# Loading and splitting the first quarter of the weights in two chunks of 128 rows

## The chip, the cores and the metric

The kernel runs on one core of one Trainium2 chip, as one launch. The metric is the device time of a run in microseconds. The median of three runs of the kernel before is 843.33 us (843.28 to 843.36). A profiled execution of the same program, taken on the same kind of chip, is what the trace shows.

## The reference, cut to what matters

Two transformer blocks are computed one after the other on 256 tokens of width 1024, all in float32. The part that the change touches is the very start: an RMS norm of the input, and the first of the products with `w_in`, a 1024 x 6144 matrix.

```python
h = concat([meta_tokens, x])                # 16 + 256 rows of 1024
a = rms_norm(h, norm_mix)
(q_na, k_na, v_na, q_hg, z_f, z_b, i_hg, g_hg, gate_na, gate_hg) = split_cols(a @ w_in)
...                                         # attention, HGRN2, gates, MLP, then two more layers
```

The first product that the kernel makes is `g_hg`, 512 columns of `w_in` that begin at column 3584.

## The kernel before, in words

Every product of the kernel is made in three matmuls on operands cut into a high and a low part: a float32 array is copied to the type float32r (the high part, a Copy on ScalarE) and the rest is the difference (the low part, a subtraction on VectorE). Weights come in units of 512 rows x 512 columns, 1 MB each, in a tile `raw` of 128 partitions x 2048 (four chunks of 128 rows side by side). `emit_raw` loads units in order on SyncE's queue (three `raw` tiles). `emit_hl` splits half a unit at a time, that is two chunks, 128 x 1024: L256 writes `whi`, L257 writes `wlo`. So a quarter of the product `g_hg`, which takes two units, is one such half. `use` hands the chunks to the matmuls.

`xstat` makes, for chunk k of the weights, the matmuls of L351 (high part of the activations, `xh`, with `whi`), L352 (`xh` with `wlo`) and L353 (low part, `xl`, with `whi`), 512 columns each. In the first unit `gh` this is done for the tokens 0 to 127 over chunks 0 to 3, then for the tokens 128 to 255 over the same chunks, then so for chunks 4 to 7.

Ahead of it stands the norm. `norm_in` squares the rows on ScalarE (L443), forms the root on GpSimd (L435) and scales on VectorE (L546). `split_in(t, g)` transposes 4 blocks of 128 x 128 of token tile t and column half g on TensorE (L411) and splits the result into `xh` (ScalarE, L418) and `xl` (VectorE, L419). The code calls these in this order:

```python
norm_in(0, h[0], 2)
first_split(1)            # half unit 0 (the first quarter): L256, L257
x00 = split_in(0, 0)
first_split(2)            # half unit 1
norm_in(1, h[1], 1, x00[:1])
split_in(1, 0)
first_split(3)
x01 = split_in(0, 1)
first_split(4)
split_in(1, 1)
```

The instructions of the whole program are then put in order by a planner, engine by engine, from priorities (the order of the code, with offsets) and a model of their durations. What it makes of a program can be seen only in a trace. The loads at the start are issued on SyncE's queue in the order of the code: the first half of `h[0]` (rows 0 to 127 of x), `grow`, its second half, `ident`, then half unit 0 (L518), `h[1]` (L519, rows 128 to 255 of x), half unit 1 (L520), half units 2 and 3 (L226), and small tables (L525 to L527), before the third unit (L226 again).

Of the kernel before, what the change touches and what calls it, by code (L numbers as in the profile page):

```python
# [11 lines left out]
AF = mybir.ActivationFunctionType  # L12
ALU = mybir.AluOpType
# [57 lines left out]
def kernel(  # L71
# [5 lines left out]
    vecs, cst, out, dbg=None,  # L77
):
    nc = tc.nc
    V, S, T, G = nc.vector, nc.scalar, nc.tensor, nc.gpsimd  # L80
# [12 lines left out]
    def nm(s):  # L93
        uid[0] += 1
        return f"{s}_{uid[0]}"
# [28 lines left out]
    def f(ap):  # L124
        return ap.bitcast(F32)
# [28 lines left out]
    units = []  # L154
# [63 lines left out]
    def emit_raw(n):  # L218
        while st["raw"] < min(n, len(units)):
            i = st["raw"]  # L220
            t = rawp.tile([128, 2048], F32, name=nm("raw"), tag="raw")
            src = units[i][1]
            d = t.rearrange("p (k n) -> p k n", n=src.shape[2])

            for k in (slice(0, 2), slice(2, 4)) if i < QD else (slice(None),):
                raw_ins[:] = [nc.sync.dma_start(out=d[:, k], in_=src[:, k])]  # L226
            raw_t[i] = t
            st["raw"] += 1


    for key, tags in BORROW.items():
        i = [u[0] for u in units].index(key)
# [10 lines left out]
    def emit_hl(i0):  # L243

        while st["hl"] < min(2 * len(units), cap[0]):
            i = st["hl"]
            if i not in borrowed and sum(k not in borrowed for k in range(i0, i)) >= NHL:
                break
            emit_raw(i // 2 + 1)
            r = raw_t[i // 2][:, 1024 * (i % 2):1024 * (i % 2) + 1024]  # L250
            if i in borrowed:
                hi, lo = (slot.tile([128, 2, 512], F32R, name=nm("wb"), tag=g) for g in borrowed[i])
            else:
                hi = hlp.tile([128, 2, 512], F32R, name=nm("whi"), tag="whi")
                lo = hlp.tile([128, 2, 512], F32R, name=nm("wlo"), tag="wlo")
            S.activation(out=hi.rearrange("p k n -> p (k n)"), in_=r, func=AF.Copy)  # L256
            V.tensor_tensor(out=lo.rearrange("p k n -> p (k n)"), in0=r,  # L257
                            in1=f(hi.rearrange("p k n -> p (k n)")), op=ALU.subtract)
            hl_t[i] = (hi, lo)
            st["hl"] += 1  # L260

# [70 lines left out]
    def use(key, budget=None):  # L332

        i = st["use"]
        assert units[i][0] == key, (units[i][0], key)
        with after(behind):
            emit_hl(2 * i)
        behind.clear()
        emit_raw(max(i, st["hl"] // 2 - NHL // 2) + NRAW)
        st["use"] += 1  # L340
        bg_step(budget or base[0], base[1])
        q = [hl_t.pop(2 * i), hl_t.pop(2 * i + 1)]
        return [(q[k // 2][0][:, k % 2], q[k // 2][1][:, k % 2]) for k in range(4)]
# [171 lines left out]
        T.matmul(g_ps[k], lhsT=one_row, rhs=grow[:, 512 * k:512 * k + 512], start=True, stop=True)  # L515
    w0 = rawp.tile([128, 2048], F32, name="raw0", tag="raw")
    w0v = w0.rearrange("p (k n) -> p k n", n=512)
    nc.sync.dma_start(out=w0v[:, 0:2], in_=units[0][1][:, 0:2])  # L518
    nc.sync.dma_start(out=h[1], in_=x[128:256])  # L519
    nc.sync.dma_start(out=w0v[:, 2:4], in_=units[0][1][:, 2:4])  # L520
    raw_t[0] = w0
# [32 lines left out]
    def first_split(n):  # L554
        cap[0] = n
        emit_hl(0)
        cap[0] = 1 << 30
# [36 lines left out]
    with after(raw_ins):  # L594
# [8 lines left out]
                    in0=vc[:, R_LB:R_LB + 16].rearrange("p (d l h) -> p d l h", d=2, l=2)[:, :, 0],  # L603
                    in1=vc[:, R_LB:R_LB + 16].rearrange("p (d l h) -> p d l h", d=2, l=2)[:, :, 1], op=ALU.subtract)
# [411 lines left out]
    for n in range(2):  # L1016
        ws = use(("yn", n))
        for t in range(2):
# [3 lines left out]
            c = slice(512 * n, 512 * n + 512)  # L1022
# [3 lines left out]
    for n in range(2):  # L1026
        ws = use(("yh", n))
        nl = len(later)
        for t in range(2):
# [3 lines left out]
            c = slice(512 * n, 512 * n + 512)  # L1033
# [331 lines left out]
    for g in range(4):  # L1365
        ps = mps()
        for b in range(2):
            for c in range(2):
                i = 2 * g + c
# [7 lines left out]
        for b in range(2):  # L1377
            k = 2 * g + b
# [353 lines left out]
```

## Time and profile before

| what | value |
|---|---|
| median of three runs | 843.33 us |
| the profiled execution, its own time | 843.46 us |
| its span, from the first to the last instruction | 841.6 us |
| TensorE (PE) busy | 827.7 us, 98% of the span |
| VectorE (DVE) busy | 577.8 us, 69% |
| ScalarE (ACT) busy | 466.6 us, 55% |
| mean rate of the DMA engines | 199 GB/s |

The profiled execution takes 1.86 us more than its span, which lies before the first and behind the last instruction. Times inside a trace count from the start of the span. A busy TensorE is not a TensorE at its peak: its matmuls overlap, so the distance from one start to the next tells more than the duration of one.

### The profile page before, as it was taken

What the parts mean: (1) busy time and instruction counts of PE and PEld (TensorE: products, weight loads), DVE (VectorE), ACT (ScalarE), POOL (GpSimd) and SP (SyncE); (2) the same over time, 40 slices, a digit from 0 to 9 for tenths busy, and PEclk for the clock granted to TensorE, in tenths of its full rate; (3) what the DMA queues carried; (4) which work ended last, traced back from release to release, by engine and by line L of the source; (5) the groups of instructions that cost most, each with busy time, mean ns of one, the idle gap of its engine ahead of it and who ended that gap; (6) DMA issues with size and microseconds to landing.
All of it is one profiled execution on the core that took longest, in us unless ns stands there. A gap on an engine that the chain in (4) does not pass through costs nothing.

```text
span 841.6 us, 13162 instructions
## 1 busy us (share of the span) xinstructions
PE 827.7 (98%) x5181; PEld 741.5 (88%) x5181; DVE 577.8 (69%) x832; ACT 466.6 (55%) x769; POOL 58.9 (7%) x139
## 2 busy tenths in 40 slices
PE   7999999999999999999999999999999999999996
PEld 5999998888889999999879989888799999898885
DVE  5746667775849976657976777876655557559753
ACT  6456755574556655544775546545566455555442
POOL 2420020001000000000021000000000000020001
PEclk9999999999999999999999999999999999999999
DMA  8863443442549997868737656757155444468521
GB/s 306 258 200 101 151 151 101 162 154 85 200 129 367 370 335 274 300 210 286 256 98 250 201 179 223 248 201 246 62 209 172 150 154 170 172 220 301 176 78 50
DMA packets 88104, 167.51 MB, mean 199 GB/s; under 512 B 4793, under 2 KB 8889, under 8 KB 88043
## 3 DMA queue, kind: packets, MB, share of 16 engines
q1 hardware_dynamic: 87371, 166.13, 57.6%
q8 instruction: 40, 0.66, 0.3%
q10 hardware_dynamic: 288, 0.52, 0.2%
q14 instruction: 21, 0.17, 0.1%
q0 software_dynamic: 384, 0.03, 0.0%
HBM read 165.62 MB, written 1.05 MB: 198 GB/s over the span
## 4 chain that ended last, share of the span: by engine, by line
PE 93%; DVE 2%; DMA 1%; ACT 1%; issue 1%; POOL 0%; SPq 0%; POOLq 0%; DVEq 0%; ACTq 0%
PE acc L353 15%; PE acc L351 15%; PE acc L352 15%; PE acc L363 9%; PE acc L362 9%; PE acc L361 9%; PE mp L363 3%; PE mp L361 3%; PE mp L362 3%; PE mp L411 2%; PE mp L881 1%; DMA raw<-in_w_in_dram 1%; PE mp L353 1%; PE mp L351 1%; DMA raw<-in_even_in_w_dram 1%
## 5 line engine op out<-in xcount | busy, mean ns | idle before, releaser
L257 DVE TENSOR_TENSOR wlo<-raw,whi 128x1024 fp32r<-128x1024 f32 x244 | 293.9, 1224 | 139.8 <-ACT whi L256 137.6
L256 ACT ACTIVATE whi<-raw 128x1024 fp32r<-128x1024 f32 x244 | 251.0, 1055 | 148.3 <-PE acc L353 90.0
L478 DVE SCALAR_TENSOR_TENSOR tb<-adw,csil,tb 128x512 f32<-128x512 f32 x96 | 71.1, 748 | 11.1 <-issue 5.8
L363 PE MATMUL acc<-oh,wlo 128*128 128x256 f32 x256 | 73.3, 287 | 0.0
L362 PE MATMUL acc<-ol,whi 128*128 128x256 f32 x256 | 73.0, 285 | 0.0
L361 PE MATMUL acc<-oh,whi 128*128 128x256 f32 x256 | 72.7, 284 | 0.0
L362 PE MATMUL acc<-xl,whi 128*128 128x272 f32 (+1 forms) x224 | 64.6, 288 | 0.0
L363 PE MATMUL acc<-xh,wlo 128*128 128x272 f32 (+1 forms) x224 | 64.5, 289 | 0.0
L361 PE MATMUL acc<-xh,whi 128*128 128x272 f32 (+1 forms) x224 | 64.3, 289 | 0.0
L361 PE MATMUL mp<-uh,whi 128*128 128x256 f32 x224 | 63.1, 285 | 0.0
L362 PE MATMUL mp<-ul,whi 128*128 128x256 f32 x224 | 63.0, 283 | 0.0
L363 PE MATMUL mp<-uh,wlo 128*128 128x256 f32 x224 | 62.1, 283 | 0.0
L351 PE MATMUL acc<-whi,hh 128*128 128x512 f32 x128 | 50.0, 392 | 0.0
L352 PE MATMUL acc<-wlo,hh 128*128 128x512 f32 x128 | 49.9, 390 | 0.0
L362 PEld LDWEIGHTS acc<-ol,whi 128*128 128x128 f32 x256 | 49.0, 191 | 0.9 <-issue 0.8
L353 PE MATMUL acc<-whi,hl 128*128 128x512 f32 x128 | 49.7, 390 | 0.0
L363 PEld LDWEIGHTS acc<-oh,wlo 128*128 128x128 f32 x256 | 49.0, 192 | 0.2
L361 PEld LDWEIGHTS acc<-oh,whi 128*128 128x128 f32 x256 | 49.0, 191 | 0.2
L351 PE MATMUL acc<-whi,yT 128*128 128x512 f32 (+1 forms) x128 | 48.5, 379 | 0.0
L352 PE MATMUL acc<-wlo,yT 128*128 128x512 f32 (+1 forms) x128 | 48.3, 377 | 0.0
L353 PE MATMUL acc<-whi,yT 128*128 128x512 f32 (+1 forms) x128 | 48.2, 377 | 0.0
L362 PEld LDWEIGHTS mp<-ul,whi 128*128 128x128 f32 x224 | 42.9, 192 | 0.1
(414 smaller groups left out, 2002.7 us busy)
## 6 DMA issues: line engine op xcount, KB each, us to landing
raw<-in_odd_in_w_dram SPq DMA_DIRECT2D x28, 1024.0 KB, 5.0
adw<-in_ada_w_dram SPq DMA_DIRECT2D x48, 512.0 KB, 6.1
raw<-in_w_in_dram SPq DMA_DIRECT2D x21, 1024.0 KB, 5.2
raw<-in_even_in_w_dram SPq DMA_DIRECT2D x20, 1024.0 KB, 5.1
raw<-in_w_up_dram SPq DMA_DIRECT2D x16, 1024.0 KB, 6.5
raw<-in_w_down_dram SPq DMA_DIRECT2D x16, 1024.0 KB, 7.3
raw<-in_even_out_w_dram SPq DMA_DIRECT2D x8, 1024.0 KB, 5.1
raw<-in_odd_out_w_dram SPq DMA_DIRECT2D x8, 1024.0 KB, 4.9
```

What stands on the lines that cost most here:

```text
L256: S.activation(out=hi.rearrange("p k n -> p (k n)"), in_=r, func=AF.Copy)
L257: V.tensor_tensor(out=lo.rearrange("p k n -> p (k n)"), in0=r, in1=f(hi.rearrange("p k n -> p (k n)")), op=ALU.subtract)
L351: T.matmul(ps, lhsT=xh, rhs=wh, start=first and k == 0, stop=False)
L352: T.matmul(ps, lhsT=xh, rhs=wl, start=False, stop=False)
L353: last_mm[:] = [T.matmul(ps, lhsT=xl, rhs=wh, start=False, stop=last and k == n - 1)]
L361: T.matmul(ps, lhsT=wh[:, c], rhs=xh, start=first and k == 0, stop=False)
L362: T.matmul(ps, lhsT=wh[:, c], rhs=xl, start=False, stop=False)
L363: T.matmul(ps, lhsT=wl[:, c], rhs=xh, start=False, stop=last and k == n - 1)
L411: last_t[:] = [T.transpose(out=ps[:, 128 * b:128 * b + 128], in_=src[:, 128 * b:128 * b + 128], identity=ident)]
L478: V.scalar_tensor_tensor(out=a, in0=w[:, k], scalar=csil[:, kk:kk + 1], in1=a, op0=ALU.mult, op1=ALU.add)
L881: T.matmul(pss[i][:, 128 * hd:128 * hd + 128], lhsT=Kc[:, hd, 128 * i:128 * i + 128], rhs=bass.AP(tensor=q.tensor, offset=q.offset, ap=ap[ ...
```

## The change

Half unit 0 is loaded by two DMAs of 128 rows (256 KB) each where one DMA brought both chunks (512 KB). They stand one behind the other on SyncE's queue, ahead of `h[1]`. Its split is made chunk by chunk: copy of chunk 0, subtraction of chunk 0, copy of chunk 1, subtraction of chunk 1, on 128 x 512 each, where one copy and one subtraction took 128 x 1024. All other half units are loaded and split as before. The tiles and their buffers are the same.

```diff
@@ emit_hl
-            S.activation(out=hi.rearrange("p k n -> p (k n)"), in_=r, func=AF.Copy)
-            V.tensor_tensor(out=lo.rearrange("p k n -> p (k n)"), in0=r,
-                            in1=f(hi.rearrange("p k n -> p (k n)")), op=ALU.subtract)
+            fh, fl = (X.rearrange("p k n -> p (k n)") for X in (hi, lo))
+
+            for c in (slice(0, 512), slice(512, 1024)) if i == 0 else (slice(0, 1024),):
+                S.activation(out=fh[:, c], in_=r[:, c], func=AF.Copy)
+                V.tensor_tensor(out=fl[:, c], in0=r[:, c], in1=f(fh[:, c]), op=ALU.subtract)
@@ the loads at the start
-    nc.sync.dma_start(out=w0v[:, 0:2], in_=units[0][1][:, 0:2])
+    for k in range(2):
+        nc.sync.dma_start(out=w0v[:, k:k + 1], in_=units[0][1][:, k:k + 1])
     nc.sync.dma_start(out=h[1], in_=x[128:256])
```

## Rows read from the trace of the kernel before

**Rows 1.** The page: TensorE's busy time, and the chain's shares by engine.
```profile
PE 827.7 (98%) x5181; PEld 741.5 (88%) x5181; DVE 577.8 (69%) x832; ACT 466.6 (55%) x769; POOL 58.9 (7%) x139
...
PE 93%; DVE 2%; DMA 1%; ACT 1%; issue 1%; POOL 0%; SPq 0%; POOLq 0%; DVEq 0%; ACTq 0%
```

**Rows 2.** Stretches: from:to, length, busy us by engine, clock, DMA share, GB/s.
```profile
24.00:402.00 378.00, 377.69 (x2469) 344.85 (x2468) 268.69 (x405) 212.30 (x381) 28.68 (x52) 1.00 0.62 212
402.00:434.00 32.00, 30.93 (x156) 25.60 (x155) 26.39 (x40) 21.07 (x39) 4.56 (x9) 1.00 0.61 202
...
596.00:609.00 13.00, 12.20 (x59) 9.12 (x57) 9.15 (x20) 8.56 (x19) 0.54 (x1) 1.00 0.00 1
```

**Rows 3.** Timeline of ScalarE: start, duration, instruction, idle time before it and releaser.
```profile
8.22 1.06 ACT L256 ACTIVATE whi<-raw 128x1024 fp32r<-128x1024 f32 x1 [2.95 <-DMA raw<-in_w_in_dram]
9.18 0.58 ACT L418 ACTIVATE xh<-mp 128x512 fp32r<-128x512 f32 x1
9.94 1.06 ACT L443 ACTIVATE junk<-h 128x1024 bf16<-128x1024 f32 x1 [0.18 <-DMA h<-in_x_dram]
...
11.21 1.06 ACT L256 ACTIVATE whi<-raw 128x1024 fp32r<-128x1024 f32 x1
...
14.43 1.06 ACT L256 ACTIVATE whi<-raw 128x1024 fp32r<-128x1024 f32 x1 [0.52 <-DMA raw<-in_w_in_dram]
15.39 1.07 ACT L418 ACTIVATE xh<-mp 128x512 fp32r<-128x512 f32 x2
```

**Rows 4.** Timeline of VectorE in the same stretch.
```profile
9.31 1.22 DVE L257 TENSOR_TENSOR wlo<-raw,whi 128x1024 fp32r<-128x1024 f32 x1 [1.59 <-ACT whi L256]
...
11.94 1.41 DVE L546 SCALAR_TENSOR_TENSOR xn<-h,sm,mp 128x512 f32<-128x512 f32 x2 [0.67 <-POOL sm L435]
13.26 3.49 DVE L257 TENSOR_TENSOR wlo<-raw,whi 128x1024 fp32r<-128x1024 f32 x3
16.67 1.28 DVE L419 TENSOR_TENSOR xl<-mp,xh 128x512 fp32r<-128x512 f32 x2
```

**Rows 5.** Timeline of TensorE in the same stretch.
```profile
9.81 0.80 PE L351 MATMUL acc<-whi,xh 128*128 128x512 f32 x1 [1.70 <-ACT xh L418]
...
12.63 0.63 PE L353 MATMUL acc<-whi,xl 128*128 128x512 f32 x1
13.06 0.63 PE L351 MATMUL acc<-whi,xh 128*128 128x512 f32 x1
13.49 1.91 PE L411 MATMUL mp<-ident,xn 128*128 128x128 f32 x8
15.05 0.78 PE L352 MATMUL acc<-wlo,xh 128*128 128x512 f32 x1
...
15.91 0.40 PE L351 MATMUL acc<-whi,xh 128*128 128x512 f32 x1
16.14 0.40 PE L352 MATMUL acc<-wlo,xh 128*128 128x512 f32 x1
...
17.89 0.48 PE L353 MATMUL acc<-whi,xl 128*128 128x512 f32 x1
```

**Rows 6.** Timeline of SyncE's queue: start and duration of an issue.
```profile
2.41 0.43 SPq L518 DMA_DIRECT2D raw<-in_w_in_dram  x1
...
6.97 0.41 SPq L527 DMA_DIRECT2D vrow<-in_pool_scale_dram  x1
8.21 2.02 SPq L226 DMA_DIRECT2D raw<-in_w_in_dram  x2
```

**Rows 7.** Groups by line and form: count, then busy us and mean ns.
```profile
L419 DVE TENSOR_TENSOR hl<-ta,hh 128x512 fp32r<-128x512 f32 x14 | 9.6, 688 | 5.1 <-ACT hh L418 5.1
...
L418 ACT ACTIVATE hh<-ta 128x512 fp32r<-128x512 f32 x14 | 8.8, 630 | 0.4
```

**Rows 8.** A stretch at the start, columns as in the second group.
```profile
4.00:6.00 2.00, 2.00 (x4) 0.66 (x2) 0.15 (x1) 0.90 (x4) 1.15 (x8) 1.00 0.73 226
```

**Rows 9.** The chain that ended last, between the two blocks: start, duration, instruction.
```profile
404.91 1.22 DVE wlo L257
```

## The prediction

> **What bounds the kernel now.** I read the page first. TensorE is busy for 827.7 us, and 93% of the chain that ended last lies on it [rows 1]. Then the table of stretches: from 24 to 402 us TensorE is busy in 377.69 of 378.00 us; in the two places where one layer ends and the next begins it lacks 32.00 - 30.93 = 1.07 us and 13.00 - 12.20 = 0.80 us [rows 2]. So behind the start TensorE works through a fixed list with next to no hole. A change at the start is worth what it moves the beginning of that unbroken stretch, and this is carried to the end if nothing behind eats it: loads there run at 212 GB/s with a DMA share of 0.62 [rows 2], so they have room.
>
> So the question is one of the first 18 us, and I read the three engines' timelines side by side. The reader is to see a ladder of gates. The first matmul starts at 9.81, released by `xh` [rows 5]. ScalarE made that `xh` at 9.18, directly behind the copy of half unit 0, which had waited 2.95 us for its load and started at 8.22 [rows 3]. VectorE then takes `wlo` at 9.31, and the rows 128 to 255 of the input, normed, at 11.94 [rows 4]. TensorE needs those for the eight transposes at 13.49, the `wlo` of half unit 1 for L352 at 15.05, and the `xl` of 16.67 for L353 at 17.89 [rows 4, 5]. Matmuls of 512 columns start 0.43 us apart at first (12.63 to 13.06) and 0.23 us apart later (15.91 to 16.14) [rows 5]: the lower and the higher of the two clock levels, 1.2 and 2.4 GHz, with TensorE at work since 9.81.
>
> **The change part by part.**
>
> *The extra DMA.* An issue costs SyncE's queue 0.43 us [rows 6]. Behind half unit 0 stand `h[1]`, half units 1 to 3 and three small tables; all are issued 0.43 us later. This lies beside transfers that are already queued: half unit 0 is issued at 2.41 and lands at 8.2 [rows 3, 6], while the engines move data all the time. The queue itself has slack: the last small issue ends at 6.97 + 0.41 = 7.38, and the next (third unit) starts only at 8.21, when half unit 0 has landed [rows 3, 6]; 0.83 us of wait take up 0.43. I take 0 for the loads behind; the bounds are 0 and 0.43 us later.
>
> *Landing.* Chunk 0 is 262 KB. At the 226 GB/s of the stretch from 4 to 6 us [rows 8] it takes 1.16 us, so it lands about 1.1 us before the whole, at 7.1. An estimate; the bounds are 5.9 us (2 x 1.16 ahead, if the second chunk waits a whole turn more) and 8.2 (both together), and the sum below does not use it, since chunk 1 stands on the path. Chunk 1 I leave at 8.2.
>
> *The Trainium skill speaks against pieces this small:* "DMA: Bandwidth & Descriptors", section "Rules for kernel authors", asks for at least 1 MiB per DMA for full bandwidth, and the section on the anatomy of one DMA fits 2.0 us plus the bytes at 436 GB/s to each. If the fixed part were paid in turn, an estimate by that page is that everything behind the second piece lands 2.0 us later. Here loads of 512 KB land at 8.22, 9.94, about 11.2 and, two pieces on, 14.43 [rows 3], about 1.6 us apart, which is less than that fixed part, so the trace does not show it paid in turn.
>
> *The split.* The forms that the change uses exist elsewhere: a copy of 128 x 512 from SBUF takes 0.630 us, the subtraction 0.688 us [rows 7]; the halves they replace take 1.06 and 1.22 us [rows 3, 4]. So ScalarE pays 2 x 0.630 - 1.06 = 0.20 us more, VectorE 2 x 0.688 - 1.22 = 0.16 us more. The first pieces lie in the time in which both engines wait for the load; only the second ones are on the path.
>
> *Gate 1.* Copy of chunk 1 at 8.22 to 8.85. Before, `xh` started 0.10 us ahead of the end of the copy (9.18 against 9.28), so now 8.75, to 9.33. First matmul 0.05 us behind that, as before: 9.38 instead of 9.81, 0.43 us earlier. Subtraction of chunk 1 at 8.88 to 9.57, `xl` of 0.68 us behind it to 10.2. The six matmuls of chunks 0 and 1, 0.43 us apart, the third not before 10.2: 9.38, 9.81, 10.2, 10.63, 11.06, 11.49. Before, the sixth started at 12.63.
>
> *Gate 2.* The seventh needs the copy of half unit 1, 11.21 + 1.06 = 12.27: 12.30 instead of 13.06. The transposes need the first half of the normed rows, 11.94 + 0.75 = 12.69: 12.73 instead of 13.49. 0.76 us earlier. These inputs come from `h[1]` (9.94) and half unit 1, which the change does not speed up.
>
> *Gate 3.* Eight transposes take TensorE 15.05 - 13.49 = 1.56 us: 14.29. L352 needs the `wlo` that VectorE starts at 13.26, one of three in 3.49 us, so to 14.42: 14.45 instead of 15.05. 0.60 us.
>
> *Gate 4.* From 15.05 to 17.89 TensorE had 2.84 us of work. From 14.45 that ends at 17.29 if the higher clock level comes as much earlier as the work. If it comes at the same moment as before, 0.60 us more of work goes at 0.43 instead of 0.23, which costs 0.60 x (1 - 0.23/0.43) = 0.28 us: 17.57. The `xl` that L353 needs is ready at 16.67 + 0.68 = 17.35, and its chain (`h[1]`, norm, three subtractions, of which the last waits for a load that landed at 14.43) is as before. So L353 starts between 17.40 and 17.57 instead of 17.89: 0.49 to 0.32 us earlier. I take 0.40. TensorE has no waits worth the name behind that [rows 2].
>
> *The sum.* 843.46 (the profiled execution) - 0.40 = 843.06. That execution stands 0.13 us above the median, so for the median 842.93, say **842.9 us**, its own range 842.5 to 843.4.
>
> What can be told from no change for this kernel is about 0.2%, 1.7 us, so 841.64 to 845.02 counts as the same. The gain is real but a quarter of that.
>
> **The rivals.**
>
> *Hidden.* If the planner puts anything else ahead of `xl` on VectorE, or L353 earlier in TensorE's list, gate 4 does not move and TensorE merely waits there: no gain, 843.3. For it: gate 4 hangs on loads and on VectorE, which the change does not touch. Against it: VectorE has no reason to run later.
>
> *The loads behind land later.* If the extra issue shifts them all by 0.43 us, gate 4 moves from 17.40 to 17.83 and 0.06 us are left: 843.3. If the second piece costs as much again as its transfer, 1.16 us, L353 starts at 18.56, 0.67 us late: 844.0. With the 2.0 us that the page of the Trainium skill would give, 1.51 us are lost, 844.8. Against it stand SyncE's 0.83 us of slack [rows 6] and the 1.6 us spacing of landings.
>
> *Slower: a new order between the blocks.* Three more instructions and other modelled times at the start can make the planner order the rest anew. The place where that hurts is 402 to 434 us: the chain leaves TensorE and goes through VectorE, on which splits of weights of 1.22 us stand between its links [rows 9]. One such split put ahead of a link delays TensorE's next layer by 1.22 us less what other work covers, and the cover is thin, since TensorE already lacks 1.07 us there [rows 2]. Two make 2.44 us, less the 0.40 gained: 843.33 + 2.04 = 845.4. It decides from the second split on. The same shuffle can gain at most the holes, 1.07 + 0.80, with the 0.40 to 841.1. For it: every engine's list hangs on the planner. Against it: all later work shifts together, so their order has little reason to change.
>
> *The change does nothing it says.* If the first matmul still waits for the whole half unit (if the two chunks land together and are copied at once), gate 1 moves by less, but ends as hidden: 843.3.
>
> **How the numbers follow.** Forecast 0.47. Hidden (with the change that does nothing) 0.16. Later loads 0.08, of which 0.02 pass the bound on the slow side. A new order 0.29: 0.10 faster, 0.14 slower, 0.05 within. So faster 0.10, the same 0.47 + 0.16 + 0.06 + 0.05 = 0.74, slower 0.14 + 0.02 = 0.16. The range holds the first three and reaches into the new orders on both sides, to the 841.1 of the holes filled and, with a little over one split lost, to 845.0.
>
> **What would show it.** In the trace after: two copies of 128 x 512 at about 7.1 and 8.2; `xh` at about 8.75; the first matmul at 9.4; the seventh at 12.3; the transposes at 12.7; L353 behind the `xl` at 17.4 to 17.6. `h[1]` should still be squared at about 9.94 and the last of the first four copies start at about 14.43; if they come 0.4 us later, the loads were delayed. If TensorE is 0.3 to 0.5 us ahead at 24 us and the end is not, something behind ate it: then the holes at 402 and 596 us have grown, and a wait for a split or a load stands there. A time outside 842.5 to 843.4 would mean that the order far from the start has changed.

## The result, and the profile after

The changed kernel takes 848.94 us (median of 4, 848.3 to 849.32); the kernel before, run beside it, 843.35 us. The ratio is 1.0064, with a 95% interval of 1.0052 to 1.0076: 5.6 us slower, where the forecast was 0.4 us faster.

The page of the changed kernel gives TensorE's work as before but for 3.3 us of longer busy time [rows 1], and a granted clock that dips in one slice near the start:

```profile
span 847.4 us, 13165 instructions
PE 831.0 (98%) x5181; PEld 744.3 (88%) x5181; DVE 577.8 (68%) x833; ACT 467.3 (55%) x770; POOL 55.1 (6%) x139
...
PEclk9899999999999999999999999999999999999999
```

I then set every instruction of TensorE beside the same one of the kernel before and followed the distance (apart from the few that changed places). From the first product's first matmul to its last it stays between -0.3 and +0.9 us, goes to +1.64 at the first matmul of the second product (L361 before, L363 after), to +3.21 at the next line's matmul, and climbs to +5.90 some 6 us later. From there to the end it stays between +5.76 and +5.96 us. So the loss is whole at 37 us, and nothing of it happens between the blocks. The timeline of TensorE around the place, in the kernel before:

```profile
22.84 0.40 PE L352 MATMUL acc<-wlo,xh 128*128 128x512 f32 x1
23.17 0.42 PE L576 MATMUL mp<-ident,xnm 16*128 16x16 f32 x4
...
26.31 0.39 PE L353 MATMUL acc<-whi,xl 128*128 128x512 f32 x1
26.54 0.54 PE L361 MATMUL acc<-xh,whi 128*128 128x272 f32 x3
26.91 0.29 PE L362 MATMUL acc<-xl,whi 128*128 128x272 f32 x1
```

and in the changed kernel (lines are 2 or 3 higher):

```profile
26.05 0.39 PE L355 MATMUL acc<-whi,xl 128*128 128x512 f32 x1
26.37 0.41 PE L579 MATMUL mp<-ident,xnm 16*128 16x16 f32 x4
...
28.18 1.06 PE L363 MATMUL acc<-xh,whi 128*128 128x272 f32 x4 [0.79 <-ACT xh L420]
30.12 0.60 PE L364 MATMUL acc<-xl,whi 128*128 128x272 f32 x1 [0.88 <-DVE xl L421]
30.52 0.43 PE L365 MATMUL acc<-xh,wlo 128*128 128x272 f32 x1
30.74 0.43 PE L363 MATMUL acc<-xh,whi 128*128 128x272 f32 x1
```

Before, the transposes of the 16 meta rows (`xnm`) stood within the first product, at 23.17, ahead of its last 10 matmuls. After, they stand behind its last one. The second product takes all 272 rows, the meta rows too, so it can't start until these are transposed and split. Before, the first half of that split (ScalarE's `xh`, VectorE's `xl`, 64 columns) was done when the first product ended:

```profile
24.23 0.22 ACT L418 ACTIVATE xh<-mp 128x64 fp32r<-128x64 f32 x1 [0.81 <-PE mp L576]
25.72 0.20 DVE L419 TENSOR_TENSOR xl<-mp,xh 128x64 fp32r<-128x64 f32 x1
```

After, ScalarE and VectorE have been given other work ahead of it. VectorE's list:

```profile
28.12 0.68 DVE L591 SCALAR_TENSOR_TENSOR gg<-gg,acc 128x512 f32<-128x512 f32 x1
28.72 1.22 DVE L260 TENSOR_TENSOR wlo<-raw,whi 128x1024 fp32r<-128x1024 f32 x1
29.85 0.22 DVE L421 TENSOR_TENSOR xl<-mp,xh 128x64 fp32r<-128x64 f32 x1
```

The 0.22 us that TensorE wants stand behind 1.22 us for weights that only the third product uses. The table of stretches (columns as in [rows 2]) shows what follows, first in the changed kernel:

```profile
26.00:28.00 2.00, 1.39 (x11) 0.78 (x9) 1.82 (x3) 1.67 (x4) 0.55 (x1) 1.00 0.73 205
28.00:30.00 2.00, 1.02 (x4) 0.61 (x4) 2.00 (x6) 0.34 (x3) 0.41 (x1) 0.85 1.05 391
30.00:32.00 2.00, 1.88 (x8) 1.88 (x9) 1.32 (x10) 0.32 (x2) 0.04 (x1) 0.50 1.17 215
32.00:34.00 2.00, 2.00 (x11) 2.00 (x10) 0.00 (x0) 0.00 (x0) 2.00 (x6) 0.50 0.89 206
34.00:36.00 2.00, 2.00 (x11) 2.00 (x11) 0.00 (x0) 0.00 (x0) 2.00 (x7) 0.50 0.99 385
36.00:38.00 2.00, 2.00 (x17) 2.00 (x17) 0.00 (x0) 0.16 (x1) 2.00 (x7) 0.94 0.04 13
```

and one stretch of the kernel before beside it:

```profile
30.00:32.00 2.00, 2.00 (x18) 2.00 (x17) 0.64 (x2) 0.00 (x0) 0.00 (x0) 1.00 0.98 194
```

The granted clock falls within the second wait (0.85 in the stretch from 28 to 30) and is 0.50, the lower level of 1.2 GHz, until about 36 us. In the 6 us behind the wait matmuls start 0.23 us apart, against 0.12 to 0.13 for the same matmuls before. That is the climb from +3.21 to +5.90: 2.7 us. TensorE looks fully busy in it; only the clock column and the counts tell. The two waits were 0.79 and 0.88 us long, with 1.06 us of matmuls between.

The start itself did not go as forecast either:

```profile
6.98 0.69 DVE L260 TENSOR_TENSOR wlo<-raw,whi 128x512 fp32r<-128x512 f32 x1 [1.31 <-ACT whi L259]
7.59 0.74 DVE L549 SCALAR_TENSOR_TENSOR xn<-h,sm,mp 128x512 f32<-128x512 f32 x1
9.03 0.69 DVE L260 TENSOR_TENSOR wlo<-raw,whi 128x512 fp32r<-128x512 f32 x1 [0.69 <-ACT whi L259]
9.64 0.74 DVE L549 SCALAR_TENSOR_TENSOR xn<-h,sm,mp 128x512 f32<-128x512 f32 x1
```

The planner put each subtraction of half unit 0 ahead of a half of the norm of rows 0 to 127. On the chip VectorE waits there for the load, the norm is late, and the first matmul starts at 10.19 instead of 9.81 [rows 5] (lines of two views, VectorE's above, TensorE's here):

```profile
8.39 1.12 PE L413 MATMUL mp<-ident,xn 128*128 128x128 f32 x4 [1.33 <-DVE xn L549]
10.19 0.79 PE L353 MATMUL acc<-whi,xh 128*128 128x512 f32 x1 [0.69 <-ACT xh L420]
```

This late start alone cost nothing: at 11.64 TensorE is 0.14 us ahead of the kernel before. It falls behind at 17 us, where it waits for an `xh` that stands behind the first copy of the third unit on ScalarE; in the kernel before that copy starts at 17.39, behind both `xh`:

```profile
16.26 1.06 ACT L259 ACTIVATE whi<-raw 128x1024 fp32r<-128x1024 f32 x1 [0.17 <-DMA raw<-in_w_in_dram]
17.22 0.58 ACT L420 ACTIVATE xh<-mp 128x512 fp32r<-128x512 f32 x1
```

```profile
17.85 0.49 PE L353 MATMUL acc<-whi,xh 128*128 128x512 f32 x1 [0.69 <-ACT xh L420]
```

The lists of the engines differ from those before only in the first 37 us, on TensorE in the place of 11 instructions, and in the one DMA. Behind that every engine does the same in the same order.

### The profile page after: what moved, and what is told of

The parts are those of the page before. It is cut to its first block, busy times and chain, and to the rows that moved or that the text cites. A ratio compares the mean times of both kernels' runs of the same rounds, so it can differ in the third digit from the quotient of the medians.

```text
span 847.4 us, 13165 instructions
## 1 busy us (share of the span) xinstructions
PE 831.0 (98%) x5181; PEld 744.3 (88%) x5181; DVE 577.8 (68%) x833; ACT 467.3 (55%) x770; POOL 55.1 (6%) x139
## 4 chain that ended last, share of the span: by engine, by line
PE 92%; DVE 3%; DMA 2%; ACT 1%; issue 1%; POOL 0%; SPq 0%; POOLq 0%; DVEq 0%; ACTq 0%
PE acc L355 14%; PE acc L353 14%; PE acc L354 14%; PE acc L364 9%; PE acc L365 9%; PE acc L363 9%; PE mp L364 3%; PE mp L363 3%; PE mp L365 3%; PE mp L413 2%; DMA raw<-in_w_in_dram 2%; PE mp L884 1%; PE mp L353 1%; PE mp L354 1%; PE mp L355 1%
## 5 line engine op out<-in xcount | busy, mean ns | idle before, releaser
L260 DVE TENSOR_TENSOR wlo<-raw,whi 128x1024 fp32r<-128x1024 f32 (+1 forms) x245 | 294.1, 1219 | 144.7 <-ACT whi L259 142.5
L259 ACT ACTIVATE whi<-raw 128x1024 fp32r<-128x1024 f32 (+1 forms) x245 | 251.4, 1052 | 150.5 <-PE acc L355 85.7
L364 PE MATMUL acc<-ol,whi 128*128 128x256 f32 x256 | 73.0, 285 | 0.0
L363 PE MATMUL acc<-oh,whi 128*128 128x256 f32 x256 | 72.7, 284 | 0.0
L364 PE MATMUL acc<-xl,whi 128*128 128x272 f32 (+1 forms) x224 | 66.2, 296 | 0.9 <-DVE xl L421 0.9
L363 PE MATMUL acc<-xh,whi 128*128 128x272 f32 (+1 forms) x224 | 65.5, 294 | 0.8 <-ACT xh L420 0.8
L363 PE MATMUL mp<-uh,whi 128*128 128x256 f32 x224 | 63.1, 285 | 0.0
L364 PE MATMUL mp<-ul,whi 128*128 128x256 f32 x224 | 63.0, 283 | 0.0
L353 PE MATMUL acc<-whi,hh 128*128 128x512 f32 x128 | 50.0, 392 | 0.0
L364 PEld LDWEIGHTS acc<-ol,whi 128*128 128x128 f32 x256 | 49.0, 191 | 0.9 <-issue 0.8
L363 PEld LDWEIGHTS acc<-oh,whi 128*128 128x128 f32 x256 | 49.0, 191 | 0.2
L353 PE MATMUL acc<-whi,yT 128*128 128x512 f32 (+1 forms) x128 | 48.5, 379 | 0.0
L364 PEld LDWEIGHTS acc<-xl,whi 128*128 128x128 f32 x224 | 43.6, 195 | 1.1 <-DVE xl L421 1.1
```

The source lines that it names most:

```text
L259: S.activation(out=fh[:, c], in_=r[:, c], func=AF.Copy)
L260: V.tensor_tensor(out=fl[:, c], in0=r[:, c], in1=f(fh[:, c]), op=ALU.subtract)
L353: T.matmul(ps, lhsT=xh, rhs=wh, start=first and k == 0, stop=False)
L363: T.matmul(ps, lhsT=wh[:, c], rhs=xh, start=first and k == 0, stop=False)
L364: T.matmul(ps, lhsT=wh[:, c], rhs=xl, start=False, stop=False)
```

## The experiments

Theory A: the loss is the late place of the meta rows in the planner's new order, in three parts: the transposes no longer fill a hole (about 1 us), the waits for their split, and the lower clock behind the waits. Theory B: it comes from what the change itself does at the start, the load in two pieces, the smaller instructions, or the chunk's subtraction ahead of the norm.

**The kernel before, with late transposes.** Nothing of the change is in it; only an edge is added, by which the transposes wait for the last matmul of the first product (`last_mm`).

```diff
         for k in range(8):
-            T.transpose(out=ps[:, 16 * k:16 * k + 16], in_=xn[2][...], identity=...)  # cut
+            with after(last_mm):
+                T.transpose(out=ps[:, 16 * k:16 * k + 16], in_=xn[2][...], identity=...)  # cut
```

> The kernel before, with one edge added: the transposes of the 16 meta rows come behind the last matmul of the first product, where the planner put them in the changed kernel. Nothing of the change is in it. Theory A (the loss is these transposes being late: waits of 0.8 and 0.9 us for the split of the meta rows, about 1 us of transposes that no longer fill a hole, and about 2.6 us because TensorE falls to its lower clock level behind the wait): 847.5 to 849.5 us. Theory B (the loss comes from the start of the changed kernel: the load in two pieces, the chunk's subtraction ahead of the norm, the splits of the third unit): 843 to 844 us.

Measured: 847.19 us, ratio 1.0048 (1.0033 to 1.0063), a little under the range of theory A. The same two waits and the same dip of the clock are there, in a kernel that loads and splits as before:

```profile
26.49 1.06 PE L361 MATMUL acc<-xh,whi 128*128 128x272 f32 x4 [0.89 <-ACT xh L418]
28.43 0.39 PE L362 MATMUL acc<-xl,whi 128*128 128x272 f32 x1 [0.87 <-DVE xl L419]
```

```profile
30.00:32.00 2.00, 2.00 (x10) 2.00 (x10) 0.00 (x0) 0.00 (x0) 1.06 (x3) 0.50 0.93 172
```

One edge alone makes 3.7 us of the 5.6. The lower clock lasted about half as long here: the distance climbed by 1.5 us instead of 2.7. What sets how long it lasts, no run shows.

**The changed kernel, with the transposes back in the first product.** The call of `meta_in` moves ahead of the last quarter of the first product, whose matmuls are put behind the transposes (`mid` is the new argument, `meta_t` holds the last transpose; cut to the two places that matter).

```diff
+                    if mid and i == 1 and t == 1:
+                        mid()
-                    with group():
+                    with group(), after(meta_t if mid and i == 1 and t == 1 else []):
                         xstat(ps[t], ...)
```

> The changed kernel, with the meta rows traced ahead of the last quarter of the first product and that quarter put behind their transposes. Theory A: the loss goes, 842.8 to 844.2 us; what is left is the first matmul at 10.2 instead of 9.8. Theory B: it stays, 847 to 849 us.

Measured: 844.43 us, ratio 1.0011 (1.0002 to 1.0021), a little above the range of theory A: 4.5 of the 5.6 us go. In the profiled execution the rest, 1.1 us, is there from 18 us on.

**The changed kernel, with the subtractions behind the norm.** `xn_last` holds the norm's last instruction.

```diff
-                V.tensor_tensor(out=fl[:, c], in0=r[:, c], in1=f(fh[:, c]), op=ALU.subtract)
+                with after(xn_last if i == 0 else []):
+                    V.tensor_tensor(out=fl[:, c], in0=r[:, c], in1=f(fh[:, c]), op=ALU.subtract)
```

> The changed kernel, with both subtractions of half unit 0 put behind the norm of the rows 0 to 127 on VectorE. The transposes of the meta rows stay late. Theory A: the first matmul moves to about 9.4, but the loss stays nearly whole, 847 to 849 us. Theory B: most of the loss goes, 843 to 844 us.

Measured: 847.61 us, ratio 1.0052 (1.0035 to 1.0069). The first matmul starts at 8.98, so the start is put right, and still 4.1 us are lost: the transposes of the meta rows are late as in the changed kernel, and the clock falls to 0.50, here too for a climb of 1.5 us:

```profile
30.00:32.00 2.00, 2.00 (x11) 2.00 (x10) 0.60 (x7) 0.00 (x0) 0.38 (x1) 0.50 1.12 204
```

The order that theory B blames on VectorE is not the large part.

**Both pins together.**

> The changed kernel with both orders: subtractions behind the norm, and the last quarter of the first product behind the transposes of the meta rows. Theory A: the order is nearly that of the kernel before, and the gain of the prediction's ladder shows, 842.7 to 843.1 us. If the ladder is wrong and the gates hide it: 843.2 to 843.6 us. Theory B with the loads as the cause: 846 us or more.

Measured: 844.18 us, ratio 1.001 (1.0001 to 1.002), outside each of the three ranges. No gain. The lead over the kernel before was 0.9 us up to 16.6 us and gone at 17.1, where a copy of the third unit, 1.06 us, stands ahead of an `xh` on ScalarE, as in the changed kernel. It is another piece of the planner's new order.

**Each part of the change alone.** First the two DMAs without the split in two, then the split in two behind one DMA.

> The kernel before with only the load of half unit 0 in two DMAs; its split stays whole, 128 x 1024. The order on every engine is that of the kernel before but for the extra issue. Theory A (the loss is the planner's new order): no change, 843.0 to 843.9 us. Theory B (two pieces make the loads behind land later): 844 us or more.

> The kernel before with only the split of half unit 0 in two; one DMA brings both chunks. The planner then puts one subtraction between the two halves of the norm on VectorE, and leaves the meta rows where they were. Theory A: 843.0 to 844.2 us, the upper end if the norm's second half waits for the load. Theory B, with the smaller instructions as the cause: 846 us or more.

Measured: 843.75 us, ratio 1.0004 (0.9995 to 1.0013), and 843.41 us, ratio 1.0001 (0.9992 to 1.001). For neither part alone can a cost be told from nothing, and in neither did TensorE's list change. Only both together turn it. So neither the load in two pieces nor the smaller instructions make the loss by themselves; of theory B the order on VectorE is left, with the 1.3 us that pinning it gave back; of these the shorter time at the lower clock makes 1.2 in the profiled executions.

**The hole filled.** 12 matmuls that nobody reads stand behind the late transposes (`meta_t` holds the last of these, `FW[0]` is a chunk of `whi`).

```diff
     meta_in()
+    with tc.high_priority(offset=40):
+        fp = mps()
+        with after(meta_t):
+            for k in range(12):
+                T.matmul(fp, lhsT=xT[0][0][:, 0, 0:128], rhs=FW[0], start=k == 0, stop=k == 11)
```

> The changed kernel with 12 more matmuls of 512 columns behind the late transposes of the meta rows, their result read by nobody, about 2.8 us at the higher clock level. They stand in the stretch in which TensorE waits in the changed kernel. If the lower clock level behind the wait is worth 2.6 us of the loss: the clock stays up, and although 2.8 us of work are added the time falls, to 846.3 to 847.8 us. If the waits alone make the loss and the clock none of it: 849 to 849.6 us.

Measured: 846.67 us against 848.94 of the changed kernel: 2.3 us faster, with 2.9 us of work more. The ratio to the kernel before is 1.0037 (1.0023 to 1.005).

```profile
26.38 3.04 PE L601 MATMUL mp<-whi,xh 128*128 128x512 f32 x12
29.25 0.27 PE L606 MATMUL mp<-ident,vrow 128*128 128x128 f32 x1
29.28 0.75 PE L363 MATMUL acc<-xh,whi 128*128 128x272 f32 x4
29.87 0.28 PE L364 MATMUL acc<-xl,whi 128*128 128x272 f32 x1
29.99 0.29 PE L365 MATMUL acc<-xh,wlo 128*128 128x272 f32 x1
```

The clock stays at 1.00 in every stretch up to 40 us, and the second product's matmuls go at 0.12 to 0.13 us from L364 on. From the last matmul of the first product to L364 it is 4.41 us here and 4.07 in the changed kernel, so nothing is gained between the two; the lead over the changed kernel is 0.25 us at L364 and 3.1 us at 37 us in the profiled executions. So the lower level is a cost of its own, beside the waits.

**The meta rows' split first, on the two other engines alone.** `behind` puts the next splits of weights behind what is in it. TensorE's list is that of the changed kernel.

```diff
-            split_bank(pv_[:, 4 * g:4 * g + 4], xT[g][0][:, :, 256:272], xT[g][1][:, :, 256:272])
+            behind.extend(split_bank(pv_[:, 4 * g:4 * g + 4], xT[g][0][:, :, 256:272], xT[g][1][:, :, 256:272]))
```

> The changed kernel; TensorE's list is left as it is, the transposes of the meta rows stay late. On ScalarE and VectorE alone the split of the meta rows is put ahead of the splits of half units 8 and 9, which the product after next is the first to use. Theory A, with waits and clock as its two large parts: L364 no longer waits until 30.1 but starts at about 28.1 (2.0 us), and the clock stays up (2.6 us): 843.9 to 845.2 us. If the loss were in TensorE's own list (the place of the transposes by itself), it would stay: 848 to 849 us. If the clock falls all the same, behind the shorter wait: 846.3 to 847.3 us.

Measured: 844.68 us, ratio 1.0015 (1.0006 to 1.0025): 4.3 us less than the changed kernel (4.1 if each is taken from the kernel before that ran with it), from the place of two copies and two subtractions. Nothing else differs in the lists of the engines.

```profile
27.63 0.76 PE L363 MATMUL acc<-xh,whi 128*128 128x272 f32 x4 [0.31 <-ACT xh L420]
28.23 0.29 PE L364 MATMUL acc<-xl,whi 128*128 128x272 f32 x1
```

L364 starts 1.9 us earlier than in the changed kernel, there is one short wait, and the clock stays up. Of the 1.5 us that are left, the profiled execution shows 1.2 by 37 us: some 0.8 from the wait at 17 us, 0.31 from the short wait. The late place of the transposes costs next to nothing in itself: they fill no hole in the kernel before, but put its matmuls off by about as much, 1.1 us, as in the late place.

**All three orders pinned.** The pins of the version with two, and `behind.extend(x01)` ahead of the first product, which holds the splits of the third unit back behind the last split of rows 0 to 127.

> The changed kernel with three orders pinned: subtractions of half unit 0 behind the norm; the splits of the third unit behind the last split of the rows 0 to 127; the last quarter of the first product behind the transposes of the meta rows. In the version with two pins the lead of 0.9 us at 16.6 was lost at 17.1, where a copy of the third unit stands ahead of xh on ScalarE. If that copy is the reason: the lead holds, 842.8 to 843.3 us beside 843.5 of the kernel before. If the later gates (the xl of the rows 128 to 255, the meta rows) eat it anyway: 843.5 to 844.3 us.

Measured: 843.27 us against 843.34 us of the kernel before, ratio 1.0002 (0.9993 to 1.0012), at the very edge of the range for a lead that holds. The start of this version:

```profile
9.35 0.79 PE L355 MATMUL acc<-whi,xh 128*128 128x512 f32 x1 [1.25 <-ACT xh L424]
...
12.07 0.54 PE L355 MATMUL acc<-whi,xh 128*128 128x512 f32 x1
12.45 1.04 PE L417 MATMUL mp<-ident,xn 128*128 128x128 f32 x8
14.15 0.50 PE L356 MATMUL acc<-wlo,xh 128*128 128x512 f32 x1 [0.67 <-DVE wlo L261]
...
17.59 0.48 PE L357 MATMUL acc<-whi,xl 128*128 128x512 f32 x1
```

Its first matmul starts 0.46 us and its L357 0.30 us earlier than in [rows 5]; the first product ends 0.3 us earlier (26.02 against 26.31). In the time of the whole kernel this can't be told from nothing. No version tried here beats the kernel before.

## Why the prediction was wrong

**The step that failed** is the assumption under the whole sum, that the order of the work stays: "all later work shifts together, so their order has little reason to change". The rival of a new order was there with 0.14 on the slow side, but at the wrong place (402 to 434 us) and for the wrong reason (splits ahead of a link between the blocks). The new order began at the start and cost most of its time between 26 and 36 us, just behind the 18 us that I read closely. I took from those rows when each instruction ran, without asking which of the places the planner could choose anew. The sign that I gave for a time outside the range, that the order far from the start has changed, was wrong too: behind 37 us the order is the old one.

**The meta rows were what moved.** In the kernel before they come within the first product and put off its other matmuls by about 1.1 us at 23.17. Pinned late, they cost 3.7 us by themselves; pinned early, they give 4.5 of the 5.6 us back. Of the distance of 5.90 us in the profiled executions, the timelines give 1.64 up to the first matmul of the second product: 0.79 is the wait for ScalarE, and the rest is the delay of 0.89 from the wait at 17 us, which did not show as long as the transposes were still to be done. The next line adds 1.57 (with the wait of 0.88 for VectorE), and the lower clock 2.69.

**The clock was weighed in the wrong direction.** Gate 4 of the prediction asked when TensorE rises to the higher level at the start. That two short stops close together let it fall again later, and that this costs as much again as the stops, was no rival. Three runs show it: 2.7 us in the changed kernel, 1.5 us in the kernel before with late transposes, and 1.5 us with the subtractions behind the norm. There was none where the hole was filled, and none where the two waits gave way to one of 0.31 us.

**Gate 1** missed for the same reason: with the planner's order the first matmul came at 10.19, not 9.38. With the order pinned it came at 9.35, where the copy of chunk 1 started at 8.18, forecast 8.22.

**Gates 2 and 3 held where the order was pinned; gate 4 did not.** In the execution with three pins the loads landed earlier than in [rows 3], so the times are to be counted from a load:

```profile
9.55 1.06 ACT L449 ACTIVATE junk<-h 128x1024 bf16<-128x1024 f32 x1 [0.26 <-DMA h<-in_x_dram]
```

From the squaring of `h[1]` (9.55 here, 9.94 before) the transposes start after 2.90 us (forecast 2.79, before 3.55), and L352's place after 4.60 us (forecast 4.51, before 5.11). L353's place, 17.59, comes after 8.04 us, where the forecast was 7.46 to 7.63 and the kernel before had 7.95: nothing is gained, and the 0.30 us by which it stands earlier in the trace lie in the loads. The prediction let L353 start as early as 0.05 us behind the first `xl`. But four transposes stand between, in the kernel before:

```profile
17.53 0.60 PE L411 MATMUL mp<-ident,xn 128*128 128x128 f32 x4
```

and in the version with three pins, where they wait for that `xl`:

```profile
16.44 1.28 DVE L425 TENSOR_TENSOR xl<-mp,xh 128x512 fp32r<-128x512 f32 x2
```

```profile
17.18 0.66 PE L417 MATMUL mp<-ident,xn 128*128 128x128 f32 x4 [0.15 <-DVE xl L425]
```

There the first `xl` ends at 16.44 + 0.68 = 17.12, and L353's place starts 0.47 us behind it. With 0.47 in place of 0.05, gate 4 of the prediction would have given 17.82, an estimate: 0.07 us earlier than before, not 0.40. So this term of the sum was wrong as well. The time does not decide it: 843.27 against 843.34, with an interval of about 0.1% to either side.

**The loads were right.** Chunk 0's copy started at 6.32, inside the bounds of 5.9 to 8.2 though earlier than the 7.1 of the estimate; chunk 1's at 8.37; the fourth half unit's at 14.54 against 14.43 [rows 3].

```profile
6.32 0.63 ACT L259 ACTIVATE whi<-raw 128x512 fp32r<-128x512 f32 x1 [0.91 <-DMA raw<-in_w_in_dram]
8.37 0.63 ACT L259 ACTIVATE whi<-raw 128x512 fp32r<-128x512 f32 x1 [1.42 <-DMA raw<-in_w_in_dram]
```

The rival of later loads is out: with the loads alone the time is 1.0004 of before. The rule of the Trainium skill on loads of at least 1 MiB ("DMA: Bandwidth & Descriptors", section "Rules for kernel authors") does not decide here; the trace shows no load behind the pieces that lands 2 us later. The fit of 2.0 us that the prediction took from the same page is given there for loads issued by GpSimd, and these are issued on SyncE's queue. The 0.02 that the prediction put beyond its bound for later loads had no price behind it: its dearest case, 844.8, lies inside.

**What stays open** is which of the planner's modelled times tips the order. It takes both parts of the change, and putting the subtractions behind the norm was not enough to bring the transposes back; the pin on the transposes was.

## What to carry to other kernels

Where a planner orders the program, cost a change at its start twice: once in the old order, and once by asking which small pieces the planner may put elsewhere, and who waits for them next. A stop of TensorE can have a second price, the time at the lower clock behind it, which a busy share hides and the clock column shows; here it was 1.5 to 2.7 us beside two stops of 1.7 to 1.8 us together. If an order matters, pin it, and look first at cheap pins: moving two copies and two subtractions back was worth some 4 us. When versions are compared gate by gate, count from the landing of the load, since that moves from one execution to the next.

## What the runs showed of the hardware that was not expected

With two waits of 0.79 and 0.88 us and 1.06 us of matmuls between, the granted clock fell to 0.50 and stayed there for about 6 us of work without a stop; in two other versions with such waits it stayed for about half as long. With single waits far apart, 1.03 us at 17 us and 0.31 us at 27 us in the version with the meta rows' split first, the clock stayed at 1.00. The same load at the start lands at different times in different executions: the first quarter's copy began at 8.22 in the kernel before [rows 3] and at 7.12 in that kernel with late transposes, where all engines have the same lists up to there. A gain of 0.4 us at the start is smaller than this.
